# A blocked cumsum, difference and matrix product: VectorE forms the passing weight sets, GpSimd the means, and some PSUM operations cover two banks

## The chip, the core and the metric

The kernel runs on one NeuronCore of a Trainium2 chip. TensorE multiplies (128 rows of a stationary tile by 512 columns at a time) into PSUM, which has eight banks of 128 x 512 f32 here. VectorE and ScalarE work on PSUM and on the on-chip memory SBUF, GpSimd on SBUF alone, and all DMAs are issued from the queue of SyncE (SP). Each engine works through its own queue in order and waits on semaphores. The metric is the device time of one execution in microseconds.

## The reference

```python
B, S, D = 8, 2048, 2048          # x: (8, 2048, 2048) f32, w: (2048, 2048) f32
cs = np.cumsum(x, axis=1)
diff = cs - np.concatenate([zeros, cs[:, :-1, :]], axis=1)
return np.matmul(diff, w)
```

The difference of the running sum is x again, so what has to be computed is x (16384 x 2048) times w (2048 x 2048), in f32 in and out.

## The kernel before

The rows of x are cut into 128 tiles of 128 rows. Tiles 0 to 3 are multiplied plainly in bf16 while w arrives. The others are taken in groups of four tiles, g, h = g + 2, g + 1 and h + 1, as the four blocks of a 2 x 2 block product that is done with seven block products in place of eight (Winograd's form of Strassen's method). The sums of blocks of x are called S1 to S4, those of w T1 to T4. In the steady groups five of the seven products, P1 to P5, are split once more in the same way (class `Quarters`): seven slots of four matmuls, P1.0 to P1.6. The other two, S2 T2 and S3 T3 for g and h, are made in 16 plain slots (`go`). A group, called a period below, has 51 slots, 204 matmuls.

Within one `Quarters` product four PSUM banks are used: `h[0]`, `h[1]`, `g[0]`, `g[1]`. Slot 0 fills h[0], ScalarE copies it to g[0] ("first", L568); slot 2 adds to h[0], ScalarE copies it out to the piece `chain` ("out2"), and VectorE adds it to h[1] into g[1] ("middle"); slot 4 adds to h[0] again ("out4"), VectorE adds that to h[1] ("last"); slots 3 and 5 add to g[0] and g[1], slot 6 to h[0]. Slots 2, 4 and 6 therefore each wait for ScalarE's copy of the one before. The left operands s1 to s4 are VectorE sums of 512 f16 columns.

The right operands are sets of four 128 x 512 f16 pieces made from w: t11, t12, t21, t22, Q1 to Q4 (class `Seven`, one object for each of the five products). Not all of them fit into SBUF. One place of 4 KB per partition, `flow`, is used in turn by the sets that are not kept: Q1 and Q4 of P1, t21 of P5, Q1 and Q3 of P3, Q1 and Q3 of P4. Four of these seven are formed anew each period by VectorE (`give`, one operation over 2048 columns); the other three, in1.Q4, in5.t21 and in4.Q3, were written to DRAM once (`spill`, L635) and are brought back each period by a DMA of 512 KB (`bring`, L639).

Each tile of x is scaled to f16: ScalarE sums the absolute values of its two halves (`weigh`, L138), VectorE adds them ("mean", L157) and takes the reciprocal ("scale", L159), ScalarE writes the scaled halves (`narrow`, L170), SP issues two transposing DMAs (`turn`, L187) and GpSimd makes the factor for the way back ("unit", L160). x is loaded through four buffers F (`load`, L130); load6.1 takes the buffer that is free when turn7.0 and turn7.1 of the period before have landed. Results leave PSUM by a ScalarE copy with a factor (`keep`, L565) and VectorE multiply-adds (`add`, L576), both over one bank of 512 columns; four result buffers go out by `put` (L584).

The order of the work is written out by hand. Every operation is recorded with a label; `emit` sorts all of them by period number times PERIOD plus the number that the table `places` gives the label, and issues them in that order, from which each engine's queue follows. Periods at the start and the end have tables of their own, the others the table `None`:

```python
def when(op):
    at, label = op[:2]
    own = places[at] if at in places else places[None]
    return at * PERIOD + own.get(label, 0)
```

Before, TensorE's slots follow one another in the steady periods so:

```
P1.0, P4.6, P2.0, P1.1, P1.2, P2.1, P2.2, P1.3, P2.3, P2.4, P1.4, P2.5, P1.5, P1.6, P5.0, P2.6, S2gT2.1.0, S2gT2.0.0, S2gT2.0.1, P5.1, P5.2, P5.3, S2gT2.1.1, P5.4, P5.5, S2hT2.0.0, P3.0, P5.6, P3.1, S2hT2.1.0, S2hT2.0.1, P3.2, P3.3, S2hT2.1.1, P3.4, P3.5, P4.0, P3.6, S3gT3.1.0, S3gT3.1.1, P4.1, S3gT3.0.0, S3gT3.0.1, P4.2, P4.3, S3hT3.1.0, S3hT3.0.0, S3hT3.0.1, P4.5, P4.4, S3hT3.1.1
```

## Time and profile before

| | us |
|---|---|
| median of 3 runs | 1472.91 |
| lowest and highest of them | 1472.23, 1476.22 |
| span of the profiled execution, first to last instruction | 1469.0 |
| TensorE busy in it | 1445.0 |
| VectorE, ScalarE, GpSimd busy | 1254.9, 1129.0, 55.1 |

The profile is of one execution; its span leaves out what lies before its first and after its last instruction, so it is a few microseconds below the times of the runs. PE is TensorE's matmuls, PEld its weight loads, DVE is VectorE, ACT ScalarE, POOL GpSimd, SP SyncE. In a row of groups stand the line, engine and operation, output and inputs, shapes, the count, then busy time in us, the mean of one in ns, and the idle time before them with what ended it. In a row of the timeline the first number is the start, the second the length in us. The ends of matmuls are modelled: consecutive matmuls of 512 columns start 0.216 us apart, while each is shown 0.379 us long, so a slot of four takes 0.863 us and its last end is shown 1.03 us after its start.

### The profile page before, as it was taken

How to read it: one execution, taken by the hardware profiler on the slowest of the kernel's cores; microseconds unless marked ns; L12 is line 12 of the kernel's file. 1: busy time of each engine (PE TensorE's matmuls, PEld its weight loads, DVE VectorE, ACT ScalarE, POOL GpSimd, SP SyncE). 2: the span in 40 equal slices, each digit the busy share in tenths (PEclk: the TensorE clock that was granted, in tenths of full speed). 3: DMA queues.
4: the chain of work that ended last, by engine and by line, in shares of the span. 5: the costliest groups of instructions: out<-in, count | busy, mean ns of one | idle time of the engine just before them, and what ended most of it. 6: DMA issues, size and time to landing. Idle time of an engine off the chain costs nothing.

```text
span 1469.0 us, 20458 instructions
## 1 busy us (share of the span) xinstructions
PE 1445.0 (98%) x6695; PEld 653.9 (45%) x6695; DVE 1254.9 (85%) x2292; ACT 1129.0 (77%) x1742; POOL 55.1 (4%) x129
## 2 busy tenths in 40 slices
PE   8999999999999999999999999999999999999998
PEld 4444444444444444444444444444444444444443
DVE  6999998888888888888888888888888888888887
ACT  5887677887777877778877777877787877787773
POOL 0000010000000000000000000000000000000000
PEclk9999999999999999999999999999999999999999
DMA  9999999999999999999999999999999999999984
GB/s 360 354 274 287 259 249 275 262 280 300 259 271 272 263 283 254 272 261 263 280 296 251 273 266 262 286 278 266 272 257 266 308 249 275 260 257 277 286 237 157
DMA packets 357130, 398.78 MB, mean 271 GB/s; under 512 B 272416, under 2 KB 272928, under 8 KB 357024
## 3 DMA queue, kind: packets, MB, share of 16 engines
q1 hardware_dynamic: 357024, 397.48, 95.3%
q8 instruction: 52, 0.85, 0.3%
q14 instruction: 54, 0.44, 0.1%
HBM read 196.61 MB, written 135.79 MB: 226 GB/s over the span
## 4 chain that ended last, share of the span: by engine, by line
PE 88%; DMA 9%; DVE 1%; ACT 1%; issue 0%; SPq 0%; DVEq 0%; ACTq 0%
PE b L551 54%; PE b L529 29%; DMA arena<-kept 6%; PE b L302 4%; DMA out_dram<-arena 2%; DMA W<-in_x_dram 1%; DVE arena L576 0%; DMA F<-in_x_dram 0%; DVE b L517 0%; PE b L260 0%; DVE arena L517 0%; PE b L430 0%; SPq L187 0%; ACT F L170 0%; ACT arena L565 0%
## 5 line engine op out<-in xcount | busy, mean ns | idle before, releaser
L529 PE MATMUL b<-W,x 128*128 128x512 f16 x2176 | 515.3, 379 | 0.0
L576 DVE SCALAR_TENSOR_TENSOR arena<-b,tiny,arena 128x512 f32<-128x512 f32 x612 | 447.7, 745 | 71.3 <-PE b L551 41.3
L551 PEld LDWEIGHTS <-arena 128*128 128x128 f16 x2700 | 263.9, 98 | 336.5 <-issue 20.5
L565 ACT ACTIVATE arena<-b,tiny 128x512 f32<-128x512 f32 x496 | 324.7, 687 | 109.3 <-DMA out_dram<-arena 85.0
L551 PE MATMUL b<-W,arena 128*128 128x512 f16 x1640 | 398.5, 379 | 3.5 <-ACT b L568 3.4
L529 PEld LDWEIGHTS <-x 128*128 128x128 f16 x2176 | 213.0, 98 | 256.7
L170 ACT ACTIVATE F<-F,tiny 128x1024 f16<-128x1024 f32 x246 | 282.8, 1150 | 11.1 <-DVE tiny L159 7.6
L551 PE MATMUL b<-W,x 128*128 128x512 f16 x1180 | 285.8, 379 | 0.2 <-ACT arena L568 0.2
L138 ACT ACTIVATE waste<-F 128x1024 uint8<-128x1024 f32 x246 | 260.5, 1059 | 29.0 <-DMA F<-in_x_dram 27.0
L551 PE MATMUL b<-arena 128*128 128x512 f16 x1060 | 258.4, 379 | 10.4 <-DMA arena<-kept 10.1
L568 ACT COPY arena<-b 128x512 f32<-128x512 f32 x294 | 168.7, 585 | 88.5 <-PE b L551 85.5
L517 DVE TENSOR_TENSOR b<-b,arena 128x512 f32<-128x512 f32 x294 | 201.4, 693 | 39.4 <-ACT arena L568 36.7
L551 PEld LDWEIGHTS <-x 128*128 128x128 f16 x1416 | 138.5, 98 | 167.5 <-issue 0.5
L568 ACT COPY b<-b 128x512 f32<-128x512 f32 x147 | 84.3, 574 | 75.4 <-PE b L551 37.4
L517 DVE TENSOR_TENSOR arena<-W 128x2048 f16<-128x2048 f16 (+1 forms) x98 | 112.9, 1154 | 20.1 <-PE b L551 19.6
L517 DVE TENSOR_TENSOR arena<-x,x 128x1024 f16<-128x1024 f16 (+1 forms) x180 | 91.8, 511 | 25.4 <-PE b L551 18.2
L160 POOL TENSOR_SCALAR tiny<-tiny 128x1 f32<-128x1 f32 x124 | 54.5, 452 | 1310.4 <-DVE tiny L157 1303.1
L517 DVE TENSOR_TENSOR x<-x,x 128x1024 f16<-128x1024 f16 x124 | 82.7, 685 | 1.1
L517 DVE TENSOR_TENSOR arena<-x,arena 128x512 f16<-128x512 f16 x118 | 47.6, 421 | 19.0 <-PE b L551 18.0
L551 PE MATMUL b<-arena,x 128*128 128x512 f16 x236 | 60.4, 379 | 0.0
L302 PE MATMUL b<-arena 128*128 128x512 bf16 x240 | 55.3, 390 | 0.8 <-DVE arena L270 0.8
L517 DVE TENSOR_TENSOR arena<-arena 128x512 f16<-128x512 f16 x116 | 48.7, 420 | 6.0 <-PE b L551 0.5
(44 smaller groups left out, 512.1 us busy)
## 6 DMA issues: line engine op xcount, KB each, us to landing
F<-in_x_dram SPq DMA_DIRECT2D x246, 512.0 KB, 6.2
out_dram<-arena SPq DMA_DIRECT2D x240, 512.0 KB, 4.8
arena<-kept SPq DMA_DIRECT2D x87, 512.0 KB, 5.7
W<-in_w_dram SPq DMA_DIRECT2D x32, 512.0 KB, 9.3
out_dram<-arena SPq DMA_DIRECT2D x32, 256.0 KB, 4.3
W<-in_x_dram SPq DMA_DIRECT2D x16, 256.0 KB, 7.4
x<-F SPq DMA_TRANSPOSE x246, 4.9
arena<-in_x_dram SPq DMA_DIRECT2D x2, 512.0 KB, 4.9
```

The lines of the kernel that those rows point to most:

```text
L138: lambda: nc.scalar.activation(waste, data, ABS, scale=1.0 / ROW, accum_out=m),
L160: record(f"unit{role(t)}", "pool", lambda: nc.gpsimd.tensor_scalar(u, m, uw, None, MUL))
L170: lambda: nc.scalar.activation(to, data, COPY, scale=s),
L302: said = nc.tensor.matmul(to[n], xP[:, r, ko, :], b[:, ds(n * NB, NB)], start=(ko == 0), stop=(ko == KO - 1),)
L517: record(label, "dve", lambda: nc.vector.tensor_tensor(dst, p, q, op))
L529: said = nc.tensor.matmul(to[n], a[k], b[k][:, n, :], start=(start and k == 0), stop=(k == KH - 1), skip_group_check=True,)
L551: said = nc.tensor.matmul(to, a[k], b[k], start=(start and k == 0), stop=(k == 3), skip_group_check=True)
L565: record(label, "act", lambda: nc.scalar.activation(c, p, COPY, scale=u))
L568: record(label, "act", lambda: nc.scalar.copy(to, p))
L576: label, "dve", lambda: nc.vector.scalar_tensor_tensor(c, p, u, c, MUL, ADD)
```

## The change

All seven passing sets are formed by VectorE: in1.Q4 is t21 - Q2, in5.t21 is Q4 + Q2, in4.Q3 is Q2 - t11, each one operation over 2048 f16 columns; the spare places of the sets are laid out so that a set is contiguous enough for it. The DRAM copies, their three writes and their 87 reads are gone. The eight PSUM banks are allocated as four pairs; C12g+X, C12h+Y, C22g+X, C22h+Y (VectorE) and keep C21g, keep C21h (ScalarE) are each one operation over the 1024 columns of both banks in place of two over one bank. The mean of each tile is taken by GpSimd, into four places in place of two. Warm-up matmuls at the start are 22 in place of 19. All tables of places are new, with PERIOD 2116.

```diff
--- before.py
+++ after.py
@@ -38,11 +38,11 @@
     TOP = 2048.0
     ROW = 4000.0
     TINY = 1e-34
-    WARM = 19
+    WARM = 22
     PLAIN = 4
     KQ = KO // 4
     END = M // P
-    PERIOD = 1589
+    PERIOD = 2116
 
     x2 = x.rearrange("b s d -> (b s) d")
     out2 = out.rearrange("b s d -> (b s) d")
@@ -61,7 +61,7 @@
     fours = Wall.bitcast(f16).rearrange("p k (i n j c) -> p k i j n c", i=4, j=2, c=NB)
     tiny = const.tile([P, 64], f32, name="tiny")
     sums_at = [tiny[:, ds(2 * i, 2)] for i in range(4)]
-    means_at = [tiny[:, ds(8 + i, 1)] for i in range(2)]
+    means_at = [tiny[:, ds(i, 1)] for i in (8, 9, 13, 14)]
     uw, uinv, wred = (tiny[:, ds(10 + i, 1)] for i in range(3))
     scales_at = [tiny[:, ds(16 + i, 1)] for i in range(8)]
     units_at = [tiny[:, ds(24 + i, 1)] for i in range(8)]
@@ -88,8 +88,10 @@
     flow = area(40, 4, f16).rearrange("p (j c) -> p j c", c=NB)
     chain = area(44, 2, f32)
     psum = ctx.enter_context(tc.tile_pool(name="ps", bufs=1, space=bass.MemoryType.PSUM))
-    banks = [psum.tile([P, NB], f32, name=f"b{i}") for i in range(8)]
+    twos = [psum.tile([P, 2, NB], f32, name=f"b{i}") for i in range(4)]
+    banks = [t[:, i, :] for t in twos for i in range(2)]
     pairs = [banks[2 * i : 2 * i + 2] for i in range(4)]
+    both = {id(p): t for p, t in zip(pairs, twos)}
 
     last = {}
 
@@ -148,13 +150,13 @@
     def scale_of(t):
         if t < END:
             m2 = sums_of.pop(t)
-            m = means_at[t % 2]
+            m = means_at[t % 4]
             s = scales[t] = scales_at[t % 8]
             u = unit[t] = units_at[t % 8]
             record(
                 f"mean{role(t)}",
-                "dve",
-                lambda: nc.vector.tensor_scalar(m, m2[:, :1], m2[:, 1:], TINY, ADD, MAX),
+                "pool",
+                lambda: nc.gpsimd.tensor_scalar(m, m2[:, :1], m2[:, 1:], TINY, ADD, MAX),
             )
             record(f"scale{role(t)}", "dve", lambda: nc.vector.reciprocal(s, m))
             record(f"unit{role(t)}", "pool", lambda: nc.gpsimd.tensor_scalar(u, m, uw, None, MUL))
@@ -505,11 +507,10 @@
             return self.all[:, ds(k * P, P)]
 
 
-    spills = ctx.enter_context(
-        tc.tile_pool(name="spills", bufs=1, space=bass.MemoryType.DRAM)
-    )
     spare = [inner[:, j, :] for j in range(4, 16)]
-    spare += [B12[k][:, n, :] for k in range(KH) for n in range(2)]
+    spare += [B12[k][:, n, :] for n in range(2) for k in range(KH)]
+    wide_spare = [inner[:, ds(4 * i, 4), :] for i in range(1, 4)]
+    wide_spare += [fours[:, ds(4 * a, 4), 1, 0, n, :] for n in range(2) for a in range(2)]
     S1 = [Part(S1_at[:, i]) for i in range(2)]
     rooms = [[Quarter(rooms_at[:, 2 * i + j, :]) for j in range(2)] for i in range(2)]
 
@@ -571,6 +572,14 @@
         for n in halves:
             add_one(f"{label}.{n}", c[:, n, :], p[n], u)
 
+    def keep_both(label, p, u):
+        c, both_p = free.pop(0), both[id(p)]
+        keep_one(label, c, both_p, u)
+        return c
+
+    def add_both(label, c, p, u):
+        add_one(label, c, both[id(p)], u)
+
     def add_one(label, c, p, u):
         record(
             label, "dve", lambda: nc.vector.scalar_tensor_tensor(c, p, u, c, MUL, ADD)
@@ -615,31 +624,20 @@
             self.t = [[t[:, k, :] for k in range(4)] for t in self.wide.values()]
             self.b = {}
 
-        def room(self):
+        def room(self, name=None):
+            self.wide[name] = wide_spare.pop(0)
             return [spare.pop(0) for _ in range(4)]
 
         def give(self, name):
 
-            p, q, op = {"Q1": ("t22", "Q2", SUB), "Q4": ("t21", "Q2", SUB), "Q3": ("Q2", "t11", SUB)}[name]
-            if name == "Q4":
-                less(f"{self.name}.{name}", passed, self.b[p], self.b[q])
-            else:
-                tensor(f"{self.name}.{name}", flow, self.wide[p], self.wide[q], op)
+            p, q, op = {
+                "Q1": ("t22", "Q2", SUB),
+                "Q3": ("Q2", "t11", SUB),
+                "Q4": ("t21", "Q2", SUB),
+                "t21": ("Q4", "Q2", ADD),
+            }[name]
+            tensor(f"{self.name}.{name}", flow, self.wide[p], self.wide[q], op)
             self.b[name] = passed
-
-        def spill(self, name):
-
-            to = self.kept = spills.tile([P, 4, NB], f16, name=f"kept{len(spilled)}")
-            spilled.append(to)
-            what = flow if self.b[name] is passed else self.wide[name]
-            record(f"{self.name}.{name}.spill", "sp", lambda: nc.sync.dma_start(to, what))
-
-        def bring(self, name):
-            kept = self.kept
-            record(f"{self.name}.{name}", "sp", lambda: nc.sync.dma_start(flow, kept))
-            self.b[name] = passed
-
-    spilled = []
 
     def make_1(i):
         t11, t12, t21, t22 = i.t
@@ -670,9 +668,8 @@
 
     def make_5(i):
         t11, t12, t21, t22 = i.t
-        i.b = dict(t21=t21)
-        i.spill("t21")
-        q, r = i.room(), i.room()
+        q, r = i.room("Q1"), i.room("Q2")
+        i.wide["Q4"] = i.wide["t21"]
         less(f"{i.name}.make1", q, t12, t11)
         less(f"{i.name}.make2", r, t22, q)
         less(f"{i.name}.make3", t12, t22, t12)
@@ -914,7 +911,7 @@
         P1.slot(0)
         P1.slot(1)
         if more:
-            in_1.bring("Q4")
+            in_1.give("Q4")
         ready["tail"]()
         P1.three()
         weigh(next_g, [0])
@@ -960,7 +957,7 @@
         P1.last()
         P1.slot(6)
         if more:
-            in_5.bring("t21")
+            in_5.give("t21")
         C11h = keep("keep C11h", Y, uh, free.pop(1))
         P2.slot(6)
         add("C11h+P2.h", C11h, P2.h, uh, [0])
@@ -978,8 +975,6 @@
         total("S4g", S4g, A12g, S2g, SUB)
         if not more:
             make_1(in_1)
-            in_1.give("Q4")
-            in_1.spill("Q4")
         go(2)
         P5.slot(2)
         P5.four()
@@ -1008,7 +1003,7 @@
         if not P5.plain:
             Ch = kept("h", P5.h, 1, uh, vh, (None, None))
         go()
-        add("C12g+X", C12g, X, ug)
+        add_both("C12g+X", C12g, X, ug)
         turn(next_g, [0])
         go()
         P5.slot(6)
@@ -1071,20 +1066,18 @@
             ready[1].one()
             ready[1].two()
         if more:
-            in_4.bring("Q3")
+            in_4.give("Q3")
         weigh(next_l, [0])
         go(2)
-        add("C12h+Y", C12h, Y, uh)
+        add_both("C12h+Y", C12h, Y, uh)
         put(C12h, h, 1)
         turn(next_k, [0])
         load(g + 8, 0)
         P4.slot(2)
-        C21g = keep("keep C21g", X, vg, halves=[0])
+        C21g = keep_both("keep C21g", X, vg)
         P4.four()
         P4.middle()
-        add("C22g+X", C22g, X, vg, [1])
-        keep("keep C21g", X, vg, C21g, [1])
-        add("C22g+X", C22g, X, vg, [0])
+        add_both("C22g+X", C22g, X, vg)
         put(C22g, g + 1, 1)
         weigh(next_l, [1])
         scale_of(next_l)
@@ -1107,18 +1100,14 @@
             ready[2].two()
         go(2)
         turn(next_l, [0])
-        C21h = keep("keep C21h", Y, vh, halves=[0])
-        add("C22h+Y", C22h, Y, vh, [0])
-        keep("keep C21h", Y, vh, C21h, [1])
-        add("C22h+Y", C22h, Y, vh, [1])
+        C21h = keep_both("keep C21h", Y, vh)
+        add_both("C22h+Y", C22h, Y, vh)
         P4.slot(6)
         turn(next_l, [1])
         put(C22h, h + 1, 1)
         load(h + 8, 0)
         if not more:
             make_3(in_4)
-            in_4.give("Q3")
-            in_4.spill("Q3")
             in_1.give("Q1")
 
         def tail():
@@ the table of the steady periods, and all others likewise @@
+            'P4.last': -1178, 'P1.0': -1109, 'P1.1': -1067, 'P1.first': -1003, 'P2.0': -990,
+            'C21h+P4.h.0': -978, 'P1.s3': -945, 'P1.2': -943, 'in1.Q4': -922, 'P2.first': -914,
+            'P1.3': -898, 'P1.out2': -886, 'C21h+P4.h.1': -872, 'P2.1': -853, 'P1.middle': -832,
+            'P2.3': -811, 'keep C11g.0': -810, 'P1.s4': -801, 'S1g': -785, 'weigh4.0': -782,
...
+            'narrow7.0': 1149, 'turn7.0': 1208, 'narrow7.1': 1248, 'turn7.1': 1318, 'put3.1': 1374,
+            'load10.0': 1397, 'unit5': 1581, 'unit7': 1594,
```

In the steady periods the queues then run in this order. TensorE, VectorE, ScalarE, SP, GpSimd:

```
P1.0, P1.1, P4.6, P2.0, P1.2, P1.3, P2.1, P2.3, P1.4, P1.5, P2.2, P1.6, P2.4, S2gT2.0.0, P2.6, S2gT2.0.1, P2.5, P5.0, S2gT2.1.0, P5.1, P5.2, P5.3, P5.4, P5.5, P5.6, S2hT2.0.0, S2hT2.0.1, S2hT2.1.0, P3.0, S2hT2.1.1, P3.1, P3.2, P3.3, S2gT2.1.1, P3.4, P3.5, S3gT3.1.0, P3.6, S3gT3.1.1, P4.0, P4.1, P4.2, S3gT3.0.0, S3hT3.1.0, P4.3, P4.4, S3gT3.0.1, P4.5, S3hT3.1.1, S3hT3.0.0, S3hT3.0.1

C21g+P4.g.0, C21g+P4.g.1, P1.s2, P2.s2, C22h+Y, scale7, C21h+P4.h.0, P1.s3, in1.Q4, C21h+P4.h.1, P1.middle, P1.s4, S1g, S3g, P2.s3, P1.last, S2g, C11g+P2.g.0, P2.middle, scale4, P2.s4, in5.t21, S1h, P5.s1, P2.last, C11g+P2.g.1, C11h+P2.h.0, P5.s2, C11h+P2.h.1, P5.s3, S3h, P5.s4, scale6, P5.middle, S2h, P4.s1, P5.last, S4h, P3.s1, P4.s2, S4g, P3.s2, in3.Q1, P3.s3, in3.Q3, P3.s4, P3.middle, C12g+X, C12g+P3.g.0, C12g+P3.g.1, scale5, P3.last, in4.Q1, C12h+P3.h.0, P1.s1, C12h+P3.h.1, C12h+Y, P4.s3, in4.Q3, P4.middle, P4.s4, in1.Q1, C22g+X, P2.s1, P4.last

keep C21h, P1.first, narrow7.0, P2.first, P1.out2, narrow7.1, keep C11g.0, weigh4.0, P1.out4, keep C11g.1, P2.out2, weigh4.1, P2.out4, narrow4.0, narrow4.1, keep C11h.1, keep C11h.0, weigh6.0, P5.first, weigh6.1, P5.out2, keep C22g.0, P5.out4, narrow6.0, keep C12g.1, narrow6.1, keep C12g.0, keep C22h.0, keep C22g.1, keep C12h.0, P3.first, keep C12h.1, keep C22h.1, weigh5.0, P3.out2, weigh5.1, P3.out4, narrow5.0, narrow5.1, P4.first, P4.out2, P4.out4, weigh7.0, keep C21g, weigh7.1

put1.0, load8.1, turn7.0, turn7.1, put3.1, load10.0, load6.1, put-1.0, load5.0, put0.0, put2.0, load5.1, turn6.0, turn4.1, turn4.0, put0.1, turn6.1, load7.0, load7.1, put2.1, load8.0, turn5.1, turn5.0, put1.1

mean4, unit5, unit7, mean6, unit6, mean5, mean7, unit4
```

At the start the order of the loads becomes first x.0.3, x.0.2, x.1.0, x.1.1, x.0.0, w.0.2, first x.0.1, x.1.2, x.1.3, w.0.0 and so on (before: w.0.2, w.0.0, w.0.3, first x.0.0, x.0.1, w.0.1), and TensorE's queue has eleven warm-up matmuls, turn x.0.1, six more, turn x.1.0, four, turn x.0.0, one, turn x.1.1 and then the first plain product (before: all 19, turn x.0.0, first plain product).

More of the change, by code (lines that the diff above doesn't have):

```diff
@@ L1142 @@
         0: {
[7 rows of a table removed]
-            'numbers turned': 35, 'zeros': 36, 'eye': 37, 'eye#2': 38, 'eye#3': 39, 'max w.0.0': 40,
[44 rows of a table removed]
-            'max w.1.14': 439, 'max w.1.15': 461, 'max': 462, 'max of all': 463, 'uw': 464,
[87 rows of a table removed]
-        },
[49 rows of a table removed]
-        },
[41 rows of a table removed]
+            'ones': -4779, 'first x.0.3': -4779, 'numbers': -4766, 'first x.0.2': -4760,
+            'numbers turned': -4753, 'first x.1.0': -4730, 'eye': -4728, 'eye#2': -4718,
[148 rows of a table added]
+        },
[46 rows of a table added]
+        },
[40 rows of a table added]
+        },
[40 rows of a table added]
+        },
[40 rows of a table added]
+        },
[40 rows of a table added]
         },
         29: {
[39 rows of a table removed]
[39 rows of a table added]
         },
         30: {
[32 rows of a table removed]
[31 rows of a table added]
         },
         31: {
-            'P4.last': -206, 'C21h+P4.h.1': -16, 'C21h+P4.h.0': 209, 'put-1.0.1': 1035,
-            'put-1.0.0': 1036,
+            'P4.last': -1117, 'C21h+P4.h.0': -1057, 'C21h+P4.h.1': -1024, 'put-1.0.0': -1016,
+            'put-1.0.1': -982,
         },
         None: {
[41 rows of a table removed]
[39 rows of a table added]
         },
```

793 rows, old and new, of the table places are left out of this document.

## The prediction

> **What bounds the kernel now.** I read the page first, then who makes TensorE wait, then the stages, then the groups and single pieces of the timeline.
>
> ```profile
> span 1469.0 us, 20458 instructions
> PE 1445.0 (98%) x6695; PEld 653.9 (45%) x6695; DVE 1254.9 (85%) x2292; ACT 1129.0 (77%) x1742; POOL 55.1 (4%) x129
> ...
> q1 hardware_dynamic: 357024, 397.48, 95.3%
> ...
> arena<-kept SPq DMA_DIRECT2D x87, 512.0 KB, 5.7
> ```
>
> TensorE is the bound: 1445.0 of 1469.0 us, so 24.0 us are all that any change of waits can win. The DMA rings are nearly full as well. The waits of TensorE:
>
> ```profile
> engine line waited for: us in total, times, longest us
> PE b L551 <- DMA arena<-kept: 10.1, 13, 1.2
> PE b L551 <- ACT b L568: 3.4, 3, 1.5
> PE b L338 <- DVE arena L229: 2.1, 1, 2.1
> PE b L260 <- DVE W L251: 1.9, 1, 1.9
> ```
>
> The sets brought back from DRAM cost TensorE 10.1 us in 13 waits; the change removes just these transfers. The stages (columns after the stage: its length, then busy time of PE, PEld, DVE, ACT, POOL, the granted clock, the DMA share, GB/s):
>
> ```profile
> 838.26:882.29 44.03, 44.03 (x206) 19.94 (x204) 37.47 (x71) 34.78 (x55) 1.49 (x4) 1.00 0.97 272
> ...
> 0.00:12.90 12.90, 8.06 (x27) 3.15 (x27) 5.81 (x12) 5.37 (x5) 0.19 (x4) 0.94 0.84 280
> 12.90:35.00 22.10, 22.09 (x132) 11.53 (x133) 18.00 (x20) 13.93 (x15) 0.00 (x0) 0.88 1.04 403
> ...
> 300.00:1320.00 1020.00, 1008.75 (x4659) 455.55 (x4658) 869.29 (x1600) 802.04 (x1258) 36.47 (x92) 1.00 0.97 271
> ```
>
> A period without a wait lasts 44.03 us: its 51 slots of four matmuls take 0.863 us each. In 1020 us only 11.25 us are lost, nine tenths of a per cent, so the steady stage has little to give and much to lose: 0.1 us more per period is 2.7 us over some 27 periods. The other 12.75 us lie at the two ends.
>
> **The change part by part.** Durations of the pieces that it touches:
>
> ```profile
> L576 DVE SCALAR_TENSOR_TENSOR arena<-b,tiny,arena 128x512 f32<-128x512 f32 x612 | 447.7, 745 | 71.3 <-PE b L551 41.3 <-ACT arena L565 22.8 <-PE b L529 4.1
> L568 ACT COPY arena<-b 128x512 f32<-128x512 f32 x294 | 168.7, 585 | 88.5 <-PE b L551 85.5 <-DMA out_dram<-arena 1.0
> L517 DVE TENSOR_TENSOR b<-b,arena 128x512 f32<-128x512 f32 x294 | 201.4, 693 | 39.4 <-ACT arena L568 36.7 <-ACT arena L565 1.3
> L517 DVE TENSOR_TENSOR arena<-W 128x2048 f16<-128x2048 f16 x90 | 109.8, 1220 | 20.1 <-PE b L551 19.6
> L517 DVE TENSOR_TENSOR x<-x,x 128x1024 f16<-128x1024 f16 x124 | 82.7, 685 | 1.1
> L157 DVE TENSOR_SCALAR tiny<-tiny 128x1 f32<-128x1 f32 x124 | 25.7, 208 | 7.4 <-ACT waste L138 6.7 <-POOL tiny L160 0.2
> L170 ACT ACTIVATE F<-F,tiny 128x1024 f16<-128x1024 f32 x246 | 282.8, 1150 | 11.1 <-DVE tiny L159 7.6
> L138 ACT ACTIVATE waste<-F 128x1024 uint8<-128x1024 f32 x246 | 260.5, 1059 | 29.0 <-DMA F<-in_x_dram 27.0
> L138 ACT ACTIVATION_READ_ACCUMULATOR waste<-F 128x1 f32 x246 | 47.7, 194 | 0.0
> ```
>
> *Transfers out.* 87 transfers of 512 KB and the three that fill them go: 47 of 397.48 MB, 12%. At the same time per byte the share of 95.3% falls to about 84% (an estimate from these two rows). Three issues per period also leave SP's queue, where each stood at the head until the passing set was free, with loads, transposes and puts behind it. Gain: the 10.1 us. Most of it is certain, because the replacement asks far less room: a transfer needs 5.7 us between two uses of the passing set, the VectorE sum 1.22 us. In the new order the gaps in slots from one reader of the passing set to the next are: Q1 to Q4 of P1 ten, Q4 to t21 of P5 ten, Q1 to Q3 of P3 four, Q1 to Q3 of P4 five. The smallest, four slots, is 3.45 us, less 1.03 for the reader to end and 1.22 for the sum: 1.2 us spare for VectorE's queue.
>
> *VectorE's load.* Three sums of 1.22 us come, 3.66 per period. Four means of 0.208 go, 0.83. Four pairs of 0.745 us become single operations over 1024 elements. No row shows one over two PSUM banks; its bounds are 0.745 (one half alone) and 1.49 (no saving). I take 1.28: from 1024 to 2048 f16 elements, two at a time, the rows go from 685 to 1220 ns, 535 for 512 steps, and 745 + 535 is 1280. That saves 0.84. VectorE goes from 37.47 to 39.5 of 44.03 us (bounds 37.3 and 40.3). It has 4.5 us free and does not become the bound by throughput. The two merged keeps on ScalarE save a few tenths; ScalarE, at 34.78, has room anyway.
>
> *The order.* This is the part that can cost. I count the new order in slots against what must happen between them, with these pieces:
>
> ```profile
> 867.61 1.03 PE L551 MATMUL b<-arena 128*128 128x512 f16 x4
> ...
> 868.67 0.59 ACT L568 COPY arena<-b 128x512 f32<-128x512 f32 x1 [1.17 <-PE b L551]
> ```
>
> ```profile
> 416.59 0.57 ACT L568 COPY b<-b 128x512 f32<-128x512 f32 x1
> ...
> 417.21 0.59 PE L551 MATMUL b<-W,arena 128*128 128x512 f16 x2
> ```
>
> A slot's end releases ScalarE 0.03 us later (867.61 + 1.03 to 868.67), and a copy releases TensorE 0.05 us after its end (416.59 + 0.57 to 417.21). So slot, copy out, next slot on the same bank takes 1.03 + 0.03 + 0.585 + 0.05 = 1.70 us. In the old order at least three slots (2.59 us) lie between such starts. The new one has five places per period with two (1.73 us): P2.2 to P2.4, P2.4 to P2.6, P5.2 to P5.4, P5.4 to P5.6, P4.0 to P4.2. They fit with 0.03 us to spare, if ScalarE stands ready: whatever is late there, TensorE loses. Bounds: 0, and 0.3 us per period (8 us in all) if one in five is hit by the tail of a 1.06 us ScalarE piece. I take 2 us: by the new ScalarE order the piece ahead of each of these copies can end 0.2 to 0.4 us before.
>
> The merged C12g+X holds S3gT3.1.0 back: three slots after S2gT2.1.1, 2.59 us, against 1.03 + 0.03 + 1.28 + 0.05 = 2.39. It fits by 0.2 us, by nothing if the operation costs 1.49. Earlier the two halves stood far from their readers. C12h+Y, C22g+X, C22h+Y have more room. I take 0, upper bound 1 us.
>
> *Means on GpSimd.* VectorE now stands at each reciprocal until GpSimd's mean is there. GpSimd's times:
>
> ```profile
> 894.92 1.32 POOL L160 TENSOR_SCALAR tiny<-tiny 128x1 f32<-128x1 f32 x2 [21.49 <-DVE tiny L157]
> ...
> 894.94 0.70 DVE L517 TENSOR_TENSOR arena<-x,x 128x1024 f16<-128x1024 f16 x1
> ```
>
> ```profile
> 918.33 0.53 POOL L160 TENSOR_SCALAR tiny<-tiny 128x1 f32<-128x1 f32 x2 [22.09 <-DVE tiny L157]
> 918.35 0.73 DVE L576 SCALAR_TENSOR_TENSOR arena<-b,tiny,arena 128x512 f32<-128x512 f32 x1
> ```
>
> Two of them take 0.53 us beside a VectorE operation on PSUM and 1.32 beside one on two SBUF tensors. So a mean is 0.28 to about 0.8 us where it was 0.21, plus a handover. Behind the waiting scale6 stands P5.middle, which P5.5 needs: P5.2 to P5.5 is three slots, 2.59 us, and 1.03 + 0.03 + 0.585 + 0.03 + 0.693 + 0.05 = 2.42 are used, so 0.17 are spare. The other three reciprocals have only early work behind them. I take 1 us in all, bounds 0 and 0.3 us per period, 8 us.
>
> The Trainium skill (SBUF — State Buffer, "Who interferes with whom") says that a VectorE instruction with two SBUF inputs and a GpSimd instruction that reads SBUF shut each other out, whoever issues first. The first pair of rows agrees. The rule adds the reverse case, a mean holding up a passing sum by up to 0.28 us; if mean6 did so ahead of P5.middle every period, that would be 7.6 us more (an estimate).
>
> *The start.* New loads and orders, 22 warm matmuls for 19.
>
> ```profile
> 2.13 7.12 PE L338 MATMUL b<-arena 128*128 128x512 bf16 x19 [2.13 <-DVE arena L229]
> 11.20 0.93 PE L260 MATMUL b<-waste,W 128*128 128x128 bf16 x8 [1.95 <-DVE W L251]
> 12.91 2.74 PE L302 MATMUL b<-arena 128*128 128x512 bf16 x6 [0.79 <-DVE arena L270]
> ```
>
> The first plain product now starts at 12.91 us. In the new order four of eight turns come before it instead of one, in time that was idle: three times 0.93 us won at most. But the first product needs w.0.0, now the tenth load and complete only 3 MB in, where today's first turn waits for 2 MB: 1 MB at 403 GB/s is 2.6 us, so it may start 1 to 2 us later. The clock of 0.88 over 22.1 us costs 2.65 us, and warm matmuls between the turns may win some of it back. I take a gain of 1 us, bounds a gain of 4 and a loss of 3.
>
> The Trainium skill (TensorE: Matmul & The Clock Gate, "What's actually happening") puts the slow clock down to an idle window of about 3.4 us. By it a start without such a gap would win the whole 2.65 us; the clocks of 0.94 and 0.88 agree that the pause before 11.20 cost speed.
>
> **The sum.** 1469.0 - 10.1 (transfers) + 2 (places two slots apart) + 0 (merged operations) + 1 (means) - 1 (start) = 1460.9 us of span. The median of the runs, 1472.91, is 3.9 above this span, so about **1465 us**. With every bound at its better end (start -4, nothing lost) it would be about 1459; with all at the worse (8 + 1 + 8 + 3 lost) about 1483.
>
> **The rivals.** *First: given back in the tight places.* The 10.1 us go, but copies two slots apart and P5.middle lose 0.2 to 0.5 us per period, 5 to 13 us: 1469 to 1477. For it: the 3.4 us of waits for copies in three hits, up to 1.5 us each, with wider spacing. Against: the periods of 44.03 us show none.
>
> *Second: slower, by one load.* In the new SP order load6.1 waits for turn7.1 to land, whose data hang on scale7 behind the merged C22h+Y. Its weigh6.1 stands on ScalarE directly ahead of P5's second copy, one of the places without room.
>
> ```profile
> 850.97 0.50 SPq L130 DMA_DIRECT2D F<-in_x_dram  x1
> ...
> DMA to landing us min/median/max: 6.3/6.3/6.3
> ...
> DMA to landing us min/median/max: 4.3/6.1/8.1
> ...
> DMA to landing us min/median/max: 3.1/4.9/7.8
> ```
>
> The rows are this load's issue and landing today, the landing of that period's eight loads, and that of the transposes. Counted from P1.0 as zero: the last slot of S3hT3 ends at 0.2; VectorE, with two adds and two sums queued ahead, reaches C22h+Y at about 1.1 and scale7 at 2.4. ScalarE may copy P1's second result only when P1.2 has ended (4.5), then narrow7.1 takes 1.15: 6.2. turn7.1 lands 4.9 later, so load6.1 issues at 11.1 and with 6.3 lands at 17.4. ScalarE wants it at 17.0 (P2.5 ends at 14.8, two adds of 0.745, P5.first of 0.57); 1.25 for weigh6.1 and 0.63 for the copy give 19.3, and P5.4 is slot 22, due at 19.0. So at today's times 0.3 us are lost per period, 8 us, 1465 + 8 - 3 = 1470; with a landing of 7.0 it is 1.0 us, 27 us, 1489. It makes the kernel slower from about 6.6 us to landing. For it: the loads of this one period reach 8.1. Against: the transfer issued just ahead (in5.t21) is gone, and 512 KB at 271 GB/s are 1.9 us, so it should land after 4.4 to 5.5.
>
> *Third: no gain.* The waits for the kept sets hide others just behind, so that only 3 to 5 of the 10.1 us come free: 1469 to 1472. The 13 waits are spread over 27 periods and the periods between run at 44.03, which speaks against it.
>
> **How the numbers follow.** About 0.3% (4.4 us) is what a measurement of this kernel can tell from no change: faster is below 1468.5, slower above 1477.3. The forecast has 0.60 (its own range 1457 to 1468.5). The first and third rivals together have 0.16 and give no change. The second has 0.24, most of it above 1477.3, near 1489 and beyond if the loads stay late, with 0.12 above 1488. Range 1456 to 1488.
>
> **What would show it.** Right: no kept rows; TensorE's waits in 300 to 1320 us under 5 us; periods of 44.03 to 44.2; VectorE near 39.5 per period; DMA share about 0.85 to 0.9; loads under 6 us to landing. Wrong: waits of TensorE on the copies of L568 or on VectorE in nearly every period, ScalarE idle for loads before P5's copies, VectorE idle for POOL, or a first plain product later than 14 us.

## The result and the profile after

The changed kernel takes **1684.86 us** (median of 3 runs, 1684.76 to 1688.05) where the kernel before takes 1472.91: a ratio of 1.1438, with a 95% interval of 1.1418 to 1.1458. Forecast were 1465 us, in a range of 1456 to 1488. The prediction was wrong, by 220 us.

The page of the kernel after:

```profile
span 1683.0 us, 20383 instructions
...
PE 1488.0 (88%) x6698; PEld 649.8 (39%) x6698; DVE 1320.0 (78%) x2130; ACT 1123.9 (67%) x1682; POOL 110.6 (7%) x253
...
q1 hardware_dynamic: 343680, 350.29, 76.4%
```

The transfers are gone: 350.29 MB instead of 397.48, and no row of kept sets. The time is lost elsewhere. TensorE does the same matmuls (and three more for warming up) and now idles for 195 us (1683.0 - 1488.0) instead of 24; that is 171 us. The other 43 of the 214 us of span are in its busy time, which rose from 1445.0 to 1488.0, as matmuls are shown longer than their spacing: a slot that the next one follows directly counts 0.86 us, one that is followed by a gap its full 1.03. Some 250 gaps at 0.17 us make these 43 us.

Who makes TensorE wait (engine, line, what it waited for; us in total, times, longest), again of the kernel after:

```profile
engine line waited for: us in total, times, longest us
PE b L552 <- ACT b L569: 78.8, 81, 1.3
PE b L552 <- DVE b L518: 65.9, 89, 1.3
PE b L552 <- ACT arena L569: 14.6, 24, 1.0
PE b L552 <- DVE arena L518: 6.7, 25, 0.5
PE b L530 <- DVE arena L585: 6.4, 26, 0.8
```

The first row is the copy "first" from bank to bank (it writes PSUM, `b`), the second VectorE's operations "middle" and "last", the third ScalarE's copies out to `chain`. 81 and 89 waits in 27 periods are about three of each of the first two kinds in every period. In the kernel before TensorE waits 3.4 us for "first", 0.2 us for copies out, and never for those two operations. The same view of VectorE and of ScalarE says what these two were waiting for:

```profile
DVE arena L518 <- PE b L552: 146.0, 117, 4.0
DVE b L518 <- PE b L552: 52.2, 89, 1.3
...
ACT arena L569 <- PE b L552: 214.8, 171, 4.3
```

The second row is the telling one. "Middle" and "last" read and write PSUM banks that no current slot touches; in the kernel before this row does not exist, and they wait for ScalarE's pieces alone (the row of L517 with `b<-b,arena` in the prediction). Now 89 of them wait for TensorE. TensorE waits for VectorE, and VectorE for TensorE. The steady stage has it all along its length (columns as in the table before):

```profile
300.00:1320.00 1020.00, 894.52 (x3994) 388.99 (x3993) 790.79 (x1268) 679.83 (x1034) 68.73 (x155) 1.00 0.76 201
```

TensorE's clock is 1.00 and the DMA share 0.76, so it is neither the clock nor the DMA rings: 125.5 us of 1020 are idle.

One place shows the mechanism, the second product P2 in the timeline of the kernel after (start, duration, engine, line, operation; in brackets the idle time before and what ended it):

```profile
806.39 0.59 ACT L569 COPY arena<-b 128x512 f32<-128x512 f32 x1 [0.17 <-PE b L552]
...
807.06 1.03 PE L552 MATMUL b<-W,arena 128*128 128x512 f16 x4
807.92 1.03 PE L530 MATMUL b<-W,x 128*128 128x512 f16 x4
...
808.18 0.70 DVE L518 TENSOR_TENSOR b<-b,arena 128x512 f32<-128x512 f32 x1 [0.87 <-PE b L552]
...
808.91 0.58 ACT L569 COPY arena<-b 128x512 f32<-128x512 f32 x1 [0.89 <-DVE b L518]
...
809.55 1.02 PE L552 MATMUL b<-arena,x 128*128 128x512 f16 x4 [0.60 <-ACT arena L569]
```

The copy "out2" of bank h0 ends at 806.98. Then P2.4 writes h0 again (807.06 to 808.09), while "middle" is to form g1 = h1 + the copy. Banks h0 and h1 are different, and "middle" has all its data from 806.98 on. Yet it starts at 808.18, when P2.4 has ended. ScalarE's copy "out4" overwrites what "middle" reads, so it starts only when that has ended (0.89 us idle), and P2.6 waits for that copy (0.60 us). These last two waits are real; the first is not. A chain slot, copy, slot has become slot, middle, copy, slot.

That wait of P2.6 belongs to the third row of TensorE's waits. The two large rows can be seen in the fifth product P5, a little later in the same view:

```profile
814.70 0.57 ACT L569 COPY b<-b 128x512 f32<-128x512 f32 x1 [0.78 <-DVE arena L585]
...
815.32 1.89 PE L552 MATMUL b<-W,arena 128*128 128x512 f16 x8 [1.29 <-ACT b L569]
...
818.16 0.70 DVE L518 TENSOR_TENSOR b<-b,arena 128x512 f32<-128x512 f32 x1 [0.35 <-ACT arena L569]
...
818.91 1.89 PE L552 MATMUL b<-W,arena 128*128 128x512 f16 x8 [0.85 <-DVE b L518]
...
820.65 0.70 DVE L518 TENSOR_TENSOR b<-b,arena 128x512 f32<-128x512 f32 x1 [0.25 <-ACT arena L569]
...
821.40 1.02 PE L552 MATMUL b<-W,arena 128*128 128x512 f16 x4 [0.60 <-DVE b L518]
```

P5.1 and P5.2 start at 815.32, when "first" (h0 to g0) has ended at 815.27. P5.2 adds to h0 and needs that; P5.1, ahead of it, writes h1 and does not. P5.4 (818.91) adds to h0 and waits for "middle", which reads h1 and writes g1; P5.6 (821.40) adds to h0 and waits for "last", which works on h1. In these three the two operations share no bank.

**Theory A.** PSUM was eight tiles of one bank and is now four tiles of two banks. The framework orders instructions by tile: work on one bank of a pair waits for work on the other. **Theory B.** The new order has no room (copies two slots apart, a late load), and that is what breaks. **Theory C.** VectorE's three sums per period and the means on GpSimd are what stalls. **Rival D.** The operations over two banks are themselves too long or too late for what stands behind them.

### The profile page after: what moved, and what is told of

Read it like the earlier page. It is cut to its first block, busy times and chain, and to the rows that moved or that the text cites. A ratio compares the mean times of both kernels' runs of the same rounds, so it can differ in the third digit from the quotient of the medians.

```text
span 1683.0 us, 20383 instructions
## 1 busy us (share of the span) xinstructions
PE 1488.0 (88%) x6698; PEld 649.8 (39%) x6698; DVE 1320.0 (78%) x2130; ACT 1123.9 (67%) x1682; POOL 110.6 (7%) x253
## 3 DMA queue, kind: packets, MB, share of 16 engines
q1 hardware_dynamic: 343680, 350.29, 76.4%
## 5 line engine op out<-in xcount | busy, mean ns | idle before, releaser
L530 PE MATMUL b<-W,x 128*128 128x512 f16 x2176 | 527.0, 379 | 8.0 <-DVE arena L585 6.4
L585 DVE SCALAR_TENSOR_TENSOR arena<-b,tiny,arena 128x1024 f32<-128x1024 f32 (+1 forms) x492 | 424.2, 878 | 97.4 <-PE b L552 46.0
L552 PE MATMUL b<-W,arena 128*128 128x512 f16 x1640 | 402.6, 379 | 90.6 <-ACT b L569 49.5
L566 ACT ACTIVATE arena<-b,tiny 128x512 f32<-128x512 f32 (+1 forms) x436 | 310.0, 742 | 124.9 <-PE b L552 42.6
L552 PE MATMUL b<-arena 128*128 128x512 f16 x1060 | 270.4, 378 | 58.5 <-ACT b L569 26.3
L552 PE MATMUL b<-W,x 128*128 128x512 f16 x1180 | 297.4, 379 | 8.5 <-ACT b L569 3.0
L518 DVE TENSOR_TENSOR arena<-W 128x2048 f16<-128x2048 f16 (+1 forms) x155 | 182.4, 1177 | 4.3 <-PE b L552 4.3
L159 POOL TENSOR_SCALAR tiny<-tiny 128x1 f32<-128x1 f32 x124 | 58.2, 469 | 1460.3 <-ACT waste L140 1074.1
L518 DVE TENSOR_TENSOR arena<-W,arena 128x2048 f16<-128x2048 f16 (+1 forms) x70 | 75.7, 1084 | 20.3 <-PE b L552 20.3
L518 DVE TENSOR_TENSOR arena<-x 128x512 f16<-128x512 f16 x118 | 49.5, 420 | 16.4 <-PE b L552 14.5
```

What stands on the lines that cost most here:

```text
L159: lambda: nc.gpsimd.tensor_scalar(m, m2[:, :1], m2[:, 1:], TINY, ADD, MAX),
L518: record(label, "dve", lambda: nc.vector.tensor_tensor(dst, p, q, op))
L530: said = nc.tensor.matmul(to[n], a[k], b[k][:, n, :], start=(start and k == 0), stop=(k == KH - 1), skip_group_check=True,)
L552: said = nc.tensor.matmul(to, a[k], b[k], start=(start and k == 0), stop=(k == 3), skip_group_check=True)
L566: record(label, "act", lambda: nc.scalar.activation(c, p, COPY, scale=u))
L585: label, "dve", lambda: nc.vector.scalar_tensor_tensor(c, p, u, c, MUL, ADD)
```

## The experiments

The ratio of each run is to the kernel before, timed beside it: 1469.2 to 1470.2 us there, where it was 1472.91 above.

**Single tiles, operations split.** The changed kernel with eight tiles; each of the six operations over two banks is two operations at the same place (add_both is shown; keep_both likewise).

```
-    twos = [psum.tile([P, 2, NB], f32, name=f"b{i}") for i in range(4)]
-    banks = [t[:, i, :] for t in twos for i in range(2)]
+    banks = [psum.tile([P, NB], f32, name=f"b{i}") for i in range(8)]
...
     def add_both(label, c, p, u):
-        add_one(label, c, both[id(p)], u)
+        def two():
+            for n in range(2):
+                said = nc.vector.scalar_tensor_tensor(c[:, n, :], p[n], u, c[:, n, :], MUL, ADD)
+            return said
+
+        record(label, "dve", two)
```

> The changed kernel with PSUM allocated as eight tiles of one bank again, as before; each of the six two-bank operations becomes two operations over one bank at the same place of the order. Sums on VectorE, means on GpSimd, warm matmuls and all places stay. Theory A (the tile of two banks makes the framework order work on one bank behind work on the other bank: the built program of the changed kernel has 557 waits between engines whose operands do not overlap in the middle half, against 64 before, and 96 in this one): nearly all of the 212 us come back, 1460 to 1480 us. Theory B (the new order has no room anywhere, so copies two slots apart stall TensorE): still 1640 to 1690. Theory C (VectorE's three sums per period and the means on GpSimd are what stalls): still above 1600, since both stay.

Measured: 1465.13 us, ratio 0.998 (0.9969 to 0.9992). All of the loss is gone, with order, places, means and sums unchanged, so theories B and C fall. The same place of P2 in the timeline of this kernel, and below it a place of P5:

```profile
844.52 0.59 ACT L567 COPY arena<-b 128x512 f32<-128x512 f32 x1 [0.17 <-PE b L550]
...
845.18 1.03 PE L550 MATMUL b<-W,arena 128*128 128x512 f16 x4
846.04 1.03 PE L528 MATMUL b<-W,x 128*128 128x512 f16 x4
846.90 1.03 PE L550 MATMUL b<-arena,x 128*128 128x512 f16 x4
...
845.27 0.69 DVE L516 TENSOR_TENSOR b<-b,arena 128x512 f32<-128x512 f32 x1
...
846.24 0.59 ACT L567 COPY arena<-b 128x512 f32<-128x512 f32 x1
...
853.93 2.75 PE L550 MATMUL b<-W,arena 128*128 128x512 f16 x12
...
853.97 0.70 DVE L516 TENSOR_TENSOR b<-b,arena 128x512 f32<-128x512 f32 x1
```

"Middle" starts at 845.27, while P2.4 (845.18 to 846.21) writes the bank beside it; "out4" follows P2.4 by 0.03 us; P2.6 starts at 846.90, without a gap. P5.4 to P5.6 (853.93) run in one piece, with "middle" of P5 beside P5.4. The chip lets both banks be worked on at once. The Trainium skill (PSUM — Partial Sum Buffer, "PSUM bank collisions raise a hardware error") makes the bank, within 32 partitions, the unit in which two engines must be kept apart; these rows, over all 128 partitions, agree that nothing asks for more than the bank.

**The allocation alone.** The kernel before, with nothing changed but four tiles of two banks.

```
-    banks = [psum.tile([P, NB], f32, name=f"b{i}") for i in range(8)]
+    twos = [psum.tile([P, 2, NB], f32, name=f"b{i}") for i in range(4)]
+    banks = [t[:, i, :] for t in twos for i in range(2)]
```

> The kernel before with one thing changed: PSUM allocated as four tiles of two banks and cut into the same eight banks. No operation, place or engine differs. Theory A: slower by 8 to 20%, 1590 to 1760 us, with the operation that adds a copy to the second bank (line 517, b<-b,arena) waiting for TensorE. Theories B and C: 1473 us within 0.3%, as nothing else is changed.

Measured: 1991.19 us, ratio 1.3561 (1.3527 to 1.3595), more than any theory expected. No operation spans two banks here, and the eight banks are cut in the order in which they were allocated. Its waits of TensorE:

```profile
PE b L552 <- DVE arena L577: 151.2, 138, 3.9
PE b L552 <- ACT b L569: 106.3, 114, 2.0
```

In the old order the adds (L577) hold TensorE up as well, with the largest row of all. A part of the loss is the clock: the granted clock of TensorE is 0.95 from 300 to 1320 us, where it is 1.00 in the kernel before and in the changed kernel. Over the run it is 0.953, and 4.7% of the 1597.9 us for which TensorE is busy make some 75 us (an estimate); what brought the clock down was not tested. Why the new order loses less than half as much was not tested; it may be that fewer of its neighbours in time share a pair.

**Two-bank tiles, operations split.** The changed kernel, with keep_both and add_both alone split as in the first experiment.

> The changed kernel with its four tiles of two banks, but each of the six two-bank operations split into two over one bank. Theory A with the allocation as the cause: within 2% of the changed kernel, 1660 to 1710 us. If instead the merged operations themselves cost the time (they need both banks finished): 1480 to 1600.

Measured: 1701.26 us in a single run, 16 us slower than with the operations merged. So under this allocation merging gains, and rival D falls as the cause of the loss. This kernel and the first experiment have the same operations in the same order, on banks of the same numbers; they differ only in how the banks are grouped into tiles, by 236 us.

**Two-bank tiles for X and Y only.** These are the pairs that the six operations need, here over two banks again.

```
+    twos = [psum.tile([P, 2, NB], f32, name=f"b{i}") for i in range(2)]
+    banks = [t[:, i, :] for t in twos for i in range(2)]
+    banks += [psum.tile([P, NB], f32, name=f"b{i}") for i in range(2, 6)]
```

> The changed kernel with two-bank tiles only for the two pairs X and Y, on which the six two-bank operations work; the other four banks are tiles of their own. 165 needless waits in the middle half instead of 557. Theory A: most of the loss goes, since P2, P3, P4 and P5 work on the other four banks; P1 alone keeps needless waits: 1470 to 1530 us. Theories B and C: 1640 to 1690.

Measured: 1473.76 us, ratio 1.0033 (1.0017 to 1.005). All that the change does to operations is in this kernel, and 211 us of the loss are not.

**X and Y in two-bank tiles, operations split.**

> Two-bank tiles for X and Y alone, as in the run before that reached 1473.8, but with the six operations over two banks split in two at their places. If the 8.6 us lost there against eight single tiles come from the waits between the banks of a tile (196 such waits here, 165 there, 96 with single tiles): 1473 to 1480, not faster than with the operations merged. If the merged operations themselves hold up what needs only one half: 1465 to 1468.

Measured: 1488.05 us, ratio 1.012 (1.0102 to 1.0139), above both expectations: the allocation of X and Y alone costs 23 us beside 1465.13, and the merged operations win 14 of them back. The first row of TensorE's waits, and one of its places in the timeline:

```profile
PE b L553 <- DVE arena L597: 9.7, 21, 0.5
```

```profile
803.72 1.41 DVE L590 SCALAR_TENSOR_TENSOR arena<-b,tiny,arena 128x512 f32<-128x512 f32 x2 [0.61 <-ACT arena L581]
...
805.22 0.57 ACT L570 COPY b<-b 128x512 f32<-128x512 f32 x1 [1.53 <-DVE tiny L162]
...
805.84 1.02 PE L553 MATMUL b<-arena 128*128 128x512 f16 x4 [0.46 <-DVE arena L597]
```

The row names an add over one bank (L597), but by the times it is another wait: P1.2 starts at 805.84, 0.05 us after P1's "first" has ended (805.79), which it needs. "First" overwrites the first bank of Y. It starts only after both halves of C22h+Y (803.72 to 805.13), though it needs the first half alone; with single tiles, in the first experiment, it starts at 837.04 when that half has ended at about 836.95 and the second half still runs.

**The other four banks in two-bank tiles.** In them P2, P5, P3 and P4 are formed; X and Y are single, and the operations split as in the first experiment.

```
+    banks = [psum.tile([P, NB], f32, name=f"b{i}") for i in range(4)]
+    twos = [psum.tile([P, 2, NB], f32, name=f"b{i}") for i in range(4, 6)]
+    banks += [t[:, i, :] for t in twos for i in range(2)]
```

> e1 again (changed order, single operations), but the four banks in which P2, P5, P3 and P4 are formed are allocated as two tiles of two banks; X and Y stay single. Theory (waits between the banks of one tile): in the built program 521 of the 620 such waits of the kernel with four two-bank tiles are here, 96 are in e1 as well; (521 - 96) / (620 - 96) of the 236 us that four two-bank tiles cost e1 make about 190 us: 1655, range 1600 to 1695. Rival (every two-bank tile costs the same, whatever runs in it): two tiles of four cost half, 118 us: 1583. Rival (the loss needs operations over two banks): no loss, 1465.

Measured: 1679.21 us, ratio 1.142 (1.1398 to 1.1443): 214 us of the 236, above the 190 expected from the count of needless waits and far from the half of the rival. With the 23 us of X and Y it makes 237, where all four together cost 236. The waits are those of the changed kernel almost to the number:

```profile
PE b L553 <- ACT b L570: 78.7, 80, 1.9
PE b L553 <- DVE b L519: 65.6, 88, 1.3
```

So the cost lies in the pairs that no operation over two banks ever touches; they were regrouped only because all eight banks were allocated alike.

**Means on VectorE.** The first experiment with the four means per period back on VectorE.

```
-                "pool",
-                lambda: nc.gpsimd.tensor_scalar(m, m2[:, :1], m2[:, 1:], TINY, ADD, MAX),
+                "dve",
+                lambda: nc.vector.tensor_scalar(m, m2[:, :1], m2[:, 1:], TINY, ADD, MAX),
```

> e1 (eight single tiles, changed order) with the four means per period back on VectorE. By the prediction's term the means on GpSimd cost 1 us: 1464, range 1463 to 1466. If VectorE's wait for a mean holds P5.middle in every period (the upper bound of that term): 1457 to 1460. If the 0.83 us per period that VectorE gets back are what it lacks: 1467 to 1472.

Measured: 1470.43 us, ratio 1.0007 (0.9995 to 1.0018), 5.3 us slower than with the means on GpSimd (on another chip; by the ratios of that run and of its repetition below, 4 to 5.4 us). The time is in the range of the third reading, by which VectorE's time counts. One stretch of the chain of work that ended last, which returns every period, shows the period's length, with the means on VectorE and, in the second fence, on GpSimd:

```profile
351.42 11.22 PE b L550 x52
...
395.61 11.22 PE b L550 x52
```

```profile
349.95 11.22 PE b L550 x52
...
394.02 11.22 PE b L550 x52
```

44.19 against 44.07 us. That is some 3 us over the steady periods; the rest is lost outside them.

**The sums alone.** The kernel before with its order, its tiles and its means, and only the transfers of kept sets replaced by sums on VectorE (the functions give, room and make_5 as in the change; no bring, no spill). Three places differ: the sum of t21 at 384.5 instead of 440, that of Q3 at 1062.5 instead of 1079, and in an early period one part of in5.make4 stands ahead of the sum that reads it.

> The kernel before, with its own order, single tiles and means, but all passing sets summed on VectorE and no transfer of kept sets; the sums of Q4 and Q3 stand about where the transfers were issued, the one of t21 a little earlier. By the prediction the 10.1 us of waits for kept sets go and little comes in their place: 1458 to 1461 beside 1469. By the third rival other waits lie just behind: 1464 to 1467. If 3.66 us more per period on VectorE do not fit the old order: 1470 to 1490.

Measured: **1462.23 us, ratio 0.9945 (0.9927 to 0.9963)**, the fastest of all; 8 us of the 10.1 predicted (5.4 to 10.7 by the interval), between the first two expected ranges. Its window of the steady stage, and the starts of the same slots in two successive periods, from the chain:

```profile
300.00:1320.00 1020.00, 1020.00 (x4708) 458.35 (x4707) 945.97 (x1684) 808.15 (x1269) 42.60 (x92) 1.00 0.88 238
```

```profile
344.93 13.81 PE b L550 x64
...
389.15 13.81 PE b L550 x64
```

In the steady stage the view shows no idle time of TensorE, where it showed 11.25 us before. But a period takes 44.22 us, 0.19 more than its 51 slots: a matmul is shown 0.16 us longer than the spacing, so gaps shorter than that stay hidden. They make some 4 us over the 23 periods of this stage. VectorE is busy 945.97 of 1020 us, about 41 of 44.22.

**Sums and means in the old order.**

> The kernel with the old order and all passing sets summed on VectorE (1462.2), and in it the four means per period on GpSimd. If the gain of 5.3 us that the means on GpSimd brought in the changed order is VectorE's time (0.83 us per period back): 1457 to 1461. If it belongs to the changed order alone, since here TensorE already waits for nothing in the steady stage: 1461.5 to 1464. If VectorE's waits for a mean fall where the old order has no room: 1465 or more.

Measured: 1463.85 us, ratio 0.9961 (0.9947 to 0.9976), no different from the sums alone within the intervals. The steady period did change, by the same slots of the chain:

```profile
350.33 13.81 PE b L550 x64
...
394.40 13.81 PE b L550 x64
```

It is 44.07 us instead of 44.22. So in the old order too the means on VectorE lengthen the period, by 0.15 us, some 3 us over the steady stage; in the new order it was 0.12. The gain does not reach the time: in the profiled run, the slowest of the six (1466.40), TensorE idles for 4.6 us from 35 to 300 us instead of 1.4, 3.5 of them in one wait for ScalarE (L430 <- ACT arena L318) that the sums alone do not have. Whether the means bring that wait about was not tested.

**The first experiment again**, beside it on the same chip.

> The changed order with eight single tiles and split operations once more, on the same chip as the run beside it: 1463 to 1467, and slower than the sums alone in the old order by 2 to 4 us.

Measured: 1465.21 us, ratio 0.997 (0.996 to 0.9981), as the first time. Beside it the kernel of the run above is 1.4 us faster; the sums alone (1462.23) were timed on another chip.

Not tried: operations over two banks while the framework keeps the two banks apart. That needs a dependence by bank inside one tile, or one written by hand.

## Why the prediction was wrong, step by step

**The step that failed** is the costing of the new allocation at nothing. The part on the order looked at the six merged operations ("I take 0, upper bound 1 us") and at the copies two slots apart, and counted for both the slots that write the bank in question. It never asked what the four two-bank tiles do to the operations that are not merged: 214 of the 236 us arise in banks where the change merges nothing. The line `twos = ...` stood in the diff, and the sum has a term for the merged operations (0) and none for the allocation. The chain it priced at 1.70 us (slot, copy, slot) took 2.49 us in the rows of P2 (807.06 to 809.55), with "middle" inside it. The text did name the sign, "waits of TensorE on the copies of L568 or on VectorE in nearly every period", but for another cause and at 5 to 13 us. Of the rivals none was right: the first named the place, at 5 to 13 us where over 200 were lost.

The other terms can be read from the experiments, where the allocation does not cover them.

**Transfers out: right, somewhat less.** Predicted -10.1, measured -8 (the sums alone). In the steady stage the 11.25 us of idle time that the view showed went; over the span it fell only from 24.0 to 15.1 us (1460.9 - 1445.8), so some 2 us came back outside that stage. The third rival (3 to 5 us) lies just outside the interval (5.4 to 10.7).

**Two-slot copies: right in kind.** Predicted +2, bounds 0 and 8. Of the five places four wait for a copy out and one, P4.2, for "first". From 300 to 1320 us of the first experiment TensorE has no wait for a copy out, and for "first" only this:

```profile
PE b L550 <- ACT b L567: 0.3, 2, 0.2
```

The period is 44.07 us, 0.04 above the slots. So the lower bound was nearly right: 0.03 us to spare was enough there. The second rival's load, load6.1, took 6.3 us to landing there (median of 22 periods; predicted 4.4 to 5.5, harmful from 6.6), longer than predicted, and yet cost TensorE nothing. Loads as a whole land after 5.7 us there and the DMA share is 0.87 in that stage, as forecast.

**Merged operations: durations right.** Groups of the kernel after:

```profile
L585 DVE SCALAR_TENSOR_TENSOR arena<-b,tiny,arena 128x1024 f32<-128x1024 f32 x120 | 153.9, 1282 | 12.0 <-ACT arena L566 7.5 <-PE b L530 1.6
...
L566 ACT ACTIVATE arena<-b,tiny 128x1024 f32<-128x1024 f32 x60 | 66.6, 1110 | 30.0 <-DVE arena L585 23.8 <-PE b L530 4.0 <-DMA out_dram<-arena 2.2
...
L159 POOL TENSOR_SCALAR tiny<-tiny 128x1 f32<-128x1 f32 x124 | 58.2, 469 | 1460.3 <-ACT waste L140 1074.1 <-issue 284.7 <-DVE arena L518 42.6
```

1282 ns were predicted as 1280. A right duration and a wrong wait: the length of an operation says nothing of what it is ordered behind.

**Means on GpSimd: wrong sign.** Predicted +1, measured -5.3 in the new order (-4 to -5.4 by the ratios) and no clear change in the old, though the period became shorter in both, by 0.12 and 0.15 us. The mean itself was in its bounds (469 ns; 0.28 to 0.8 us predicted). What was left out is that work stands behind VectorE's queue even where its throughput suffices. A sign of it, in the new order: the copies "first" of ScalarE wait 23.3 us for the split adds of VectorE with the means on GpSimd, and 29.8 with the means on VectorE. That this makes the whole difference is not shown. From the Trainium skill (SBUF — State Buffer, "Who interferes with whom") the prediction had estimated that a mean could hold up the passing sums for 7.6 us; the runs show a gain, so that case does not decide here.

**The start: no gain.** Predicted -1. The kernel after begins its first plain product at 14.69 us, where it was 12.91:

```profile
13.66 0.61 PE L262 MATMUL b<-waste,W 128*128 128x128 bf16 x8 [1.61 <-DVE arena L272]
14.69 2.53 PE L304 MATMUL b<-arena 128*128 128x512 bf16 x11 [0.42 <-ACT arena L289]
...
71.10 0.59 PE L304 MATMUL b<-arena 128*128 128x512 bf16 x2
```

Its clock is better (windows):

```profile
0.00:12.90 12.90, 7.91 (x46) 3.71 (x46) 5.55 (x13) 3.24 (x3) 0.19 (x4) 1.00 0.82 272
12.90:35.00 22.10, 19.01 (x109) 9.41 (x110) 15.95 (x17) 15.96 (x16) 0.00 (x0) 1.00 1.03 398
```

1.00 where it was 0.94 and 0.88. The two nearly cancel: the last plain matmul ends at 71.69 against 70.58 us, and as one slot of the next product (0.86) now stands ahead of it, the kernel after is some 0.3 us behind (an estimate from these rows). The first product came 1.8 us later, within the 1 to 2 of the prediction, and the clock was won; what was not counted is that TensorE then idles for 3.1 us of the second window, where it idled for 0.01 before. The Trainium skill (TensorE: Matmul & The Clock Gate, "What's actually happening") puts the slow clock down to an idle window of about 3.4 us; the pause that the prediction held to be the cause was 1.95 us, and the first experiment and the one with the means on VectorE, with the same order at the start and gaps of at most 1.5 us, show clocks of 0.92 and 1.00 from 12.90 to 35 us, so the rule does not say which of the two will come.

**Why 1465 came out after all in the first experiment.** It isn't that every term held. Steps that the runs show: sums on VectorE -8 (1470.2 to 1462.2); the new order and start +8 (1462.2 to 1470.4, means on VectorE in both); means on GpSimd -5 (to 1465.1). Differences of 2 or 3 us between runs on different chips are not read here. The +8 is not in the steady periods, which take 44.19 us in the new order and 44.22 in the old, with the means on VectorE in both. From 35 to 300 us, where the first periods lie, with tables of their own, TensorE is busy for 259.1 us instead of 263.6; the rest was not placed. The prediction had counted the steady order alone: +2 for it, -1 for the start and +1 for the means, where the runs show +8 for the first two together and -5 for the third. These misses cancelled; the time that came out right was luck in that part.

## What to carry to other kernels

A tile is also the unit of ordering: before banks, halves or slices are put into one tile, list for each pair of engines what they do at the same time in the two parts, for every tile that is regrouped, not only where an operation will use the whole. Here the two pairs that gained merged operations cost 9 us of 1465 with them, and the two that were regrouped only for uniformity cost 214. And a diff is read by its declarations too: a changed allocation has a price for every instruction that names the buffer.

## What was not expected

The framework, and not the chip, made these waits; in the trace they look like any other wait of an engine for an engine. The sign by which they can be told is a wait between operations with no data in common: "middle" ended its wait with the end of a matmul into the neighbouring bank (808.18 after 808.09). In the built program of the changed order with split operations, counted over half of the periods, 620 waits between engines join operations that share no data when the tiles have two banks, 96 when they are single, and 521 when only the pairs of P2 to P5 have two.

The size of the loss does not follow the number of such waits alone. The 425 more of the pairs of P2 to P5 (521 instead of 96) cost 214 us, the 100 more of X and Y (196 instead of 96) only 23. And the same regrouping costs 236 us in the new order and 522 us (1991.2 to 1469.2) in the old one, some 75 of them by the lower clock.
